# Key copies by GpSimd, sums of weight quarters kept in DRAM, and four more products in plain float32, in a decoder-layer kernel

## The chip, the cores and the metric

The kernel runs on one core of one Trainium2 chip. The metric is device time in microseconds (us) of one launch; lower is better. The result must agree with a float32 reference.

## The reference, cut to what matters

One layer over 2048 tokens of width 1024, all in float32. `IN_COLS` is 3072, `HEAD_DIM` 64, `D_FF` 4096.

```python
def hybrid_mixer(h, w_in, conv_w, g_attn_out, g_conv_out, w_out):
    proj = h @ w_in
    q, k, v, bg, cg, xc = jnp.split(proj, 6, axis=-1)          # 8 heads of 64
    for window, dilation in ((128, 1), (512, 4), (2048, 16)):
        o, lse = dilated_window_attention(q, k, v, window, dilation)
        outs.append(o); lses.append(lse)
    mix_w = jax.nn.softmax(jnp.stack(lses, axis=0), axis=0)
    attn = jnp.einsum('pbsh,pbshe->bshe', mix_w, jnp.stack(outs, axis=0))
    conv = short_gated_conv(bg, cg, xc, conv_w)
    return jnp.concatenate([rms_norm(attn), rms_norm(conv)], -1) @ w_out
# x += hybrid_mixer(rms_norm(x)); x += memory_cross_attention(rms_norm(x), mem)
# x += squared_relu(rms_norm(x) @ w_up) @ w_down; final rms_norm
```

Every query attends, in each of the three patterns, to a band of keys in its own block and in the block before. The three outputs are mixed by a softmax over the logarithms of their denominators.

## The kernel before, in words

**Products of matrices.** The large products are cut into *groups*, one for a weight block of 1024x1024 and one half of the tokens (1024). A group does 7 products of quarters instead of 8 (a Strassen-Winograd scheme): some of its operands are sums or differences of quarters. Each product is 4 *steps*, one for each tile of 128 rows, so a group has 28 steps. The order of the products in a group is 1, 2, 6, 7, 4, 5, 3. Group names: -2 to 3 are the input projection (`vg`, `ux`, `qk` for the first token half, then the same three for the second), 6 and 7 are `w` (the output projection), 8 and 9 are `s`, 10 and 11 are `o`, 12 and above are the MLP. Groups of one weight block for the two token halves (-2 and 1, -1 and 2, 0 and 3, 6 and 7, 10 and 11) have the same left operand; 8 and 9 have the same right operand, which is computed.

**Split and plain steps.** In a split step each operand is cut into a high part (by ScalarE: `w_hi` L206, `o_hi` L271) and the remainder (by VectorE: `w_lo` L213, `o_lo` L282), and TensorE does 12 matmuls of 128x512 in a fast float32 form (L385; L380 where two tiles of 256 are done). A product in the table `WHOLE` does 4 matmuls in plain float32 instead (L401, or L397) and needs no cut; the profile records each of these as two rows. Before the change `WHOLE` holds products 1 and 2 of group -2.

**Sums of quarters.** `w_sum` (L215 to L226) and `o_sum` (L228 to L244) form them on VectorE, in each group anew, each over 128x1024, into the loaded page or into a small buffer. `w_load` (L166 to L180) loads the four quarters of a group's weights, a page each of [128, 4, 512] (1 MB), from a ring of 20 pages.

**Order.** The tables `WSUM` and `OSUM` and the lists `plan` and `post` say before or after which step each such job is written; each engine then runs what was written for it in that order. `later(d, job)` writes a job d *ticks* on; there is a tick after each step and, in attention, after each unit. All transfers are issued by SyncE (SP), in the order in which they were written.

**Attention** (from L744) runs between groups 3 and 6: 4 pairs of heads, for each pair the patterns 2, 1, 0 and for each pattern 16 units, so 48 units a pair. A unit makes scores (matmuls L790 and L791, which read query pages and key pages), masks (VectorE L802), exponentials (ScalarE L813), transposes (L830) and outputs (L847). `qk` writes the loads of the next pair: `load_q` L703, `load_k` L726 to L731, `load_v` L736. A key page holds the same 64 rows twice, in partitions 0 to 63 and 64 to 127, since the high and low parts of the queries stand in the two halves. `load_k` fetches them twice from DRAM (L729 and L731, 512 KB each); only for pair 0 the second half is a VectorE copy (`dup_k` L734). `order_q` (L709) copies queries into the order of another pattern, on GpSimd (POOL, L717), ScalarE or VectorE.

**Combination.** After a pair, `combine` mixes its three outputs while the next pair runs: weights are computed (L893 to L902), stored to DRAM (`btd`, L905), loaded back broadcast over partitions for each quarter `tb` of the tokens (L927, L928), and GpSimd does five products and sums of 128x512 for each quarter (L917); the result is stored by `dma` L422. The delays are those of `combine`, L933 to L945.

Of the kernel before, what the change touches and what calls it, by code (L numbers as in the profile page):

```python
# [50 lines left out]
def _body(tc, a, out):  # L51
# [108 lines left out]
    WHOLE = {(-2, 1), (-2, 2)}  # L160
# [21 lines left out]
    def w_src(g, p, m):  # L182
        if p in (6, 3):
            return S2_[m // 2][:, m % 2]
        return WQ[g, *{1: (0, 0), 2: (0, 1), 7: (0, 0), 4: (1, 1), 5: (1, 0)}[p]][:, m]
# [41 lines left out]

    def o_sum(g, i, m):  # L228
# [15 lines left out]
        dve.tensor_tensor(to, x, y, op)  # L244

    def o_src2(g, p, m):
        if KEEP[g] and p in (7, 4, 5):
# [4 lines left out]

    def o_hi(o, m):
# [772 lines left out]
    for j in range(16):  # L1026
# [440 lines left out]
```

## Time and profile before

| | before |
|---|---|
| median of 3 runs | 2682.17 us (2678.83 to 2685.64) |
| profiled execution | 2685.0 us, its span 2682.8 us |
| TensorE busy | 2614.5 us, 97% |
| VectorE busy | 2259.4 us, 84% |
| ScalarE busy | 1458.1 us, 54% |
| GpSimd busy | 116.6 us, 4% |

A share of 97% says that TensorE has work nearly always; it is an average over stages. Where it falls in one stage, the timeline of TensorE (PE) shows the gap and, in brackets behind a row, how long the engine was idle and which instruction ended the wait. PEclk is the clock that TensorE was granted, as a share of full speed. DMA share is the mean busy share of the 16 DMA engines. A step's time is the distance between the starts of its first matmul and the next step's.

### The profile page before, as it was taken

To read this page: it belongs to the slowest core of one execution; us is meant where nothing else is said; L and a number is where in the kernel's file an instruction comes from. 1 tells how busy PE (TensorE), PEld (TensorE's weight loads), DVE (VectorE), ACT (ScalarE), POOL (GpSimd) and SP (SyncE) were. 2 spreads that over 40 slices of the span, in tenths; PEclk is the share of its full clock that TensorE was granted. 3 is DMA by queue.
4 is the path that set the end of the run, shared out by engine and by line. 5 is a ranking of instruction groups with operands and counts; after the bars stand their busy time and mean duration, and the time that the engine had idled before them with its cause. 6 is when DMAs were issued, how large, how long until landed. Compare 5 with 4: busy or idle time off the path is not lost.

```text
span 2682.8 us, 35255 instructions
## 1 busy us (share of the span) xinstructions
PE 2614.5 (97%) x13350; PEld 2171.2 (81%) x13350; DVE 2259.4 (84%) x3469; ACT 1458.1 (54%) x2466; POOL 116.6 (4%) x133
## 2 busy tenths in 40 slices
PE   8999999989889999999999999999999999999998
PEld 6888888878778677888888888888887888888886
DVE  6989889768676699998999887879789987978788
ACT  5545555358666344677545546364554636355563
POOL 0000000001344200000000000000000000000000
PEclk9999999999989999999999999999999999999999
DMA  4736443895787944355563211111121511111111
GB/s 162 232 104 210 153 166 134 269 262 119 178 186 220 306 166 158 110 188 189 205 218 110 95 63 63 63 63 63 48 94 48 188 63 64 63 33 55 56 47 63
DMA packets 196680, 353.91 MB, mean 132 GB/s; under 512 B 21024, under 2 KB 76704, under 8 KB 186912
## 3 DMA queue, kind: packets, MB, share of 16 engines
q1 hardware_dynamic: 195968, 351.15, 41.6%
q8 instruction: 105, 1.72, 0.3%
q14 instruction: 63, 0.52, 0.1%
q10 hardware_dynamic: 544, 0.52, 0.1%
HBM read 264.53 MB, written 87.10 MB: 131 GB/s over the span
## 4 chain that ended last, share of the span: by engine, by line
PE 63%; DVE 22%; DMA 9%; issue 3%; ACT 2%; SPq 1%; POOL 1%; DVEq 0%; ACTq 0%; POOLq 0%
PE ps L385 54%; DVE pg L282 4%; DVE w L213 4%; DMA w<-btd 2%; DMA pg<-qkd 2%; PE ps L847 2%; PE ps L380 1%; DVE s L39 1%; PE ps L790 1%; PE ps L830 1%; DVE pg L1089 1%; PE ps L791 1%; DVE pg L244 1%; PE ps L112 1%; DVE pg L219 1%
## 5 line engine op out<-in xcount | busy, mean ns | idle before, releaser
L385 PE MATMUL ps<-pg,w 128*128 128x512 f32 x9036 | 2080.8, 391 | 20.7 <-DVE pg L282 16.2
L385 PEld LDWEIGHTS ps<-pg,w 128*128 128x128 f32 x9036 | 1692.2, 188 | 380.0 <-DVE pg L282 25.0
L206 ACT ACTIVATE w<-pg 128x1024 fp32r<-128x1024 f32 x276 | 290.9, 1054 | 271.4 <-PE ps L385 235.9
L282 DVE TENSOR_TENSOR pg<-pg 128x1024 fp32r<-128x1024 f32 x308 | 375.2, 1220 | 3.6 <-ACT pg L271 3.2
L213 DVE TENSOR_TENSOR w<-pg,w 128x1024 fp32r<-128x1024 f32 x276 | 336.5, 1219 | 47.6 <-ACT w L206 47.3
L271 ACT ACTIVATE pg<-pg 128x1024 fp32r<-128x1024 f32 x308 | 314.1, 1046 | 37.4 <-DVE pg L500 13.3
L813 ACT ACTIVATE s<-s,stat 128x256 f32<-128x256 f32 (+1 forms) x384 | 172.6, 451 | 75.5 <-DVE stat L802 75.0
L1212 DVE TENSOR_TENSOR pg<-ps,pg 128x512 f32<-128x512 f32 x223 | 151.8, 684 | 49.0 <-PE ps L385 49.0
L206 ACT ACTIVATE w<-s 128x1024 fp32r<-128x1024 f32 x112 | 117.9, 1053 | 134.4 <-PE ps L385 78.3
L412 ACT ACTIVATE s<-pg 128x1024 f32<-128x1024 f32 x79 | 83.3, 1056 | 186.1 <-DVE pg L1089 111.4
L802 DVE CUSTOM_DVE_ANT_0 s<-ps,w 128x256 f32<-128x256 f32 (+1 forms) x344 | 108.9, 370 | 47.9 <-PE ps L791 42.6
L213 DVE TENSOR_TENSOR w<-s,w 128x1024 fp32r<-128x1024 f32 x112 | 136.1, 1215 | 2.4 <-ACT w L206 2.4
L244 DVE TENSOR_TENSOR pg<-pg 128x1024 f32<-128x1024 f32 x112 | 136.3, 1217 | 1.0
L1183 DVE TENSOR_TENSOR pg<-ps,pg 128x512 f32<-128x512 f32 x96 | 65.9, 687 | 77.6 <-PE ps L385 77.6
L790 PE MATMUL ps<-pg 128*128 128x256 f32 x384 | 108.3, 313 | 10.8 <-DMA pg<-qkd 8.9
L791 PE MATMUL ps<-pg 128*128 128x256 f32 x384 | 98.4, 287 | 12.1 <-DMA pg<-qkd 8.4
L1184 ACT ACTIVATE pg<-pg 128x512 f32<-128x512 f32 x96 | 60.6, 631 | 80.9 <-DVE pg L1183 80.8
L1178 ACT ACTIVATE pg<-ps 128x512 f32<-128x512 f32 x96 | 56.7, 596 | 86.1 <-PE ps L385 85.5
L282 DVE TENSOR_TENSOR pg<-s,pg 128x1024 fp32r<-128x1024 f32 x78 | 94.5, 1219 | 9.7 <-ACT pg L271 9.6
L833 DVE COPY s<-ps 128x256 f32<-128x256 f32 (+1 forms) x192 | 100.9, 566 | 1.3 <-PE ps L830 0.7
L271 ACT ACTIVATE pg<-s 128x1024 fp32r<-128x1024 f32 x78 | 82.0, 1052 | 33.2 <-DVE s L244 33.2
L790 PEld LDWEIGHTS ps<-pg 128*128 128x128 f32 x384 | 73.7, 192 | 27.2 <-issue 15.1
(158 smaller groups left out, 2422.8 us busy)
## 6 DMA issues: line engine op xcount, KB each, us to landing
pg<-w_up SPq DMA_DIRECT2D x32, 1024.0 KB
pg<-w_down SPq DMA_DIRECT2D x32, 1024.0 KB
pg<-qkd SPq DMA_DIRECT2D x44, 512.0 KB
pg<-w_in SPq DMA_DIRECT2D x21, 1024.0 KB
pg<-xT SPq DMA_DIRECT2D x19, 1024.0 KB
qkd<-pg SPq DMA_DIRECT2D x64, 256.0 KB
pg<-x2d SPq DMA_DIRECT2D x16, 1024.0 KB
vd<-pg SPq DMA_DIRECT2D x96, 128.0 KB
```

The costliest lines, as they stand in the source:

```text
L206: act.activation(hi, src, AF.Copy)
L213: dve.tensor_tensor(lo, src, f(hi), OP.subtract)
L244: dve.tensor_tensor(to, x, y, op)
L271: act.activation(hi, src, AF.Copy)
L282: dve.tensor_tensor(lo, src, f(hi), OP.subtract)
L385: pe.matmul(ps, wt[l][:, m % 2, k * 128:k * 128 + 128], o[x][:, k, cols], start=k == 0 and j == 0 and p in (1, 2, 5), stop=k == 3 and j == ...
L790: pe.matmul(Sh, qv, kv[0], start=True, stop=False)
L791: pe.matmul(Sh, qv, kv[1], start=False, stop=True)
L802: dve.tensor_tensor_reduce(smv, sv, mv, -0.125, 3e38, OP.add, OP.min, mt[:, c1:c1 + 1])
L813: act.activation(pout, pin, AF.Exp, bias=mt[:, c1:c1 + 1], scale=-1.0, accum_out=zt[:, c1:c1 + 1])
L833: dve.tensor_copy(t_.rearrange("p i h q -> p (i h q)")[:, :w], pt[:, :w])
L1212: dve.tensor_tensor(y, ps, y, OP.add)
```

## The change

Four things are changed.

1. **Sums kept in DRAM.** For the groups in `LSUM` (keys: the second token half; values: the first) and `RSUM` (group 9 from 8), the first group stores the four sums of quarters (`smd`, 1 MB for each) as it forms them, and the second group loads seven pages, one for each product (`s_load`, `t_load`), instead of four, and forms no sums of that operand. 24 MB are stored and 24 sum pages loaded more; 18 more pages in all, as 6 quarters are no longer needed. 48 VectorE sums (40 in `w_sum`, 8 in `o_sum`) are gone.
2. **Plain float32.** `WHOLE` takes in (0, 2), (6, 2), (6, 4) and (19, 4): 16 steps. Their cuts, 4 on VectorE and 4 on ScalarE for each product, are gone.
3. **Keys.** For pairs 1 to 3 a key page is loaded once, into partitions 0 to 63, and GpSimd copies it into the other half in four pieces of 64x512, written 6 ticks after the load. The four key loads are written at (pattern 1, units 5, 12, 15) and (pattern 0, unit 1) instead of (1, 10), (1, 13), (0, 1), (0, 4); the queries at (2, 12) instead of (1, 2); the values of the next pair's first pattern at (0, 6) instead of (1, 2).
4. **Combination.** Its delays are shorter: weights at 7, 8, 9 instead of 8, 10, 12, store at 10 instead of 14, loads of quarter `tb` at 11 + 5 tb instead of 15 + 5 tb, the products 3 ticks behind their loads instead of 2, the stores 11 + tb instead of 8.

Line numbers behind the change: L385 is L416, L401 is L433, L206 is L205, L213 is L212, L271 is L298, L282 is L309, L244 is L264, L219 is L218, L717 is L750, L917 is L954, L927 is L964, L729 is L762, L738 is L773, L422 is L455; the copy of keys is L769.

```diff
+    LSUM, RSUM = {1: -2, 2: -1, 3: 0, 7: 6, 11: 10}, {9: 8}
+    smd = {g: {p: dp.tile([128, 4, 512], F32, name=f"smd{g + 2}_{p}") for p in ((4, 5, 6, 7) if g == 8 else (3, 5, 6, 7))} for g in (-2, -1, 0, 6, 8, 10)}
...
-    WHOLE = {(-2, 1), (-2, 2)}
+    WHOLE = {(-2, 1), (-2, 2), (0, 2), (6, 2), (6, 4), (19, 4)}
...
     def w_src2(g, p, m):
+        if g in LSUM and p in (6, 7, 5, 3):
+            return WQ[g, p][:, m:m + 2]
...
+        if g in LSUM.values():
+            if i in (2, 4):
+                later(1, dma, smd[g][6 if i == 2 else 3][:, 2 * m:2 * m + 2], S2_[m])
+            elif m == 1:
+                later(1, dma, smd[g][7 if i == 3 else 5], WQ[g, 0, 0] if i == 3 else WQ[g, 1, 0])
+
+    def s_load(g, p):
+        if p in (1, 2, 4):
+            w_load(g, *{1: (0, 0), 2: (0, 1), 4: (1, 1)}[p])
+        else:
+            WQ[g, p] = page([128, 4, 512])
+            sp.dma_start(WQ[g, p], smd[LSUM[g]][p])
...
+            if g + 1 in LSUM:
+                for i, p in enumerate(order):
+                    after(28 * g + 18 + 4 * i, s_load, g + 1, p)
+            else:
+                for d, q in ((13, (0, 0)), (19, (1, 1)), (21, (1, 0)), (22, (0, 1))):
+                    after(28 * g + d, w_load, g + 1, *q)
...
         sp.dma_start(f(t_[0:64]), src)
-        if pr:
-            sp.dma_start(f(t_[64:128]), src)
-
-    def dup_k(h, i):
-        dve.tensor_copy(K[0, h, i][64:128], f(K[0, h, i][0:64]))
+
+    def dup_k(pr, h, i, eng=pool):
+
+        t_ = K[pr, h, i]
+        for b in range(1 if eng is dve else 4):
+            cs = slice(0, T) if eng is dve else slice(b * 512, b * 512 + 512)
+            eng.tensor_copy(t_[64:128, cs], f(t_[0:64, cs]))
...
-        kj = {(1, 10): 0, (1, 13): 1, (0, 1): 2, (0, 4): 3}.get((pat, b))
+        kj = {(1, 5): 0, (1, 12): 1, (1, 15): 2, (0, 1): 3}.get((pat, b))
         if kj is not None and pr < 3:
             load_k(pr + 1, kj // 2, kj % 2)
+            later(6, dup_k, pr + 1, kj // 2, kj % 2)
...
-            later((4, 5, 5)[i] if last else 8 + 2 * i, comb_w, pr, i, eng)
-        later(6 if last else 14, comb_bt, pr)
+            later((4, 5, 5)[i] if last else 7 + i, comb_w, pr, i, eng)
+        later(6 if last else 10, comb_bt, pr)
...
-                later(15 + 5 * tb, comb_ldb, pr, tb, pool, 2, 8)
+                later(11 + 5 * tb, comb_ldb, pr, tb, pool, 3, 11 + tb)
```

On GpSimd, while pair 1 runs and the keys of pair 2 come, the last two quarters of the combination of pair 0 (`w_...` are the broadcast weights) stand before the change ahead of the reordering of queries for pair 2:

```order
L917 TENSOR_TENSOR pg<-pg,w_5879 128x512 x2
L917 TENSOR_TENSOR pg<-pg 128x512
L917 TENSOR_TENSOR pg<-pg,w_5880 128x512
L917 TENSOR_TENSOR pg<-pg 128x512
L917 TENSOR_TENSOR pg<-pg,w_5979 128x512 x2
L917 TENSOR_TENSOR pg<-pg 128x512
L917 TENSOR_TENSOR pg<-pg,w_5980 128x512
L917 TENSOR_TENSOR pg<-pg 128x512
L717 CAST pg<-pg 128x4x4x32 x6
```

Behind it the same place reads, from the copies of the first key page on:

```order
L769 CAST pg<-pg 64x512 x4
L954 TENSOR_TENSOR pg<-pg,w_5783 128x512 x2
L954 TENSOR_TENSOR pg<-pg 128x512
L954 TENSOR_TENSOR pg<-pg,w_5784 128x512
L954 TENSOR_TENSOR pg<-pg 128x512
L954 TENSOR_TENSOR pg<-pg,w_5887 128x512 x2
L954 TENSOR_TENSOR pg<-pg 128x512
L954 TENSOR_TENSOR pg<-pg,w_5888 128x512
L954 TENSOR_TENSOR pg<-pg 128x512
L769 CAST pg<-pg 64x512 x12
L750 CAST pg<-pg 128x4x4x32 x6
```

The copies of the other three key pages stand behind the last products and ahead of the queries' reordering.

On SP, in the same pair, the key loads stand before between the loads of the third and fourth quarter of the combination and behind a store of its result (L422):

```order
L729 DMA pg<-qkd 64x2048
L731 DMA pg<-qkd 64x2048
L422 DMA atd<-pg 128x512
L927 DMA w_5979<-btd 64x2x512
L928 DMA w_5980<-btd 64x512
L927 DMA w_5979<-btd 64x2x512
L928 DMA w_5980<-btd 64x512
L729 DMA pg<-qkd 64x2048
L731 DMA pg<-qkd 64x2048
L422 DMA atd<-pg 128x512
L729 DMA pg<-qkd 64x2048
L731 DMA pg<-qkd 64x2048
```

Behind the change:

```order
L455 DMA atd<-pg 128x512
L964 DMA w_5887<-btd 64x2x512
L965 DMA w_5888<-btd 64x512
L964 DMA w_5887<-btd 64x2x512
L965 DMA w_5888<-btd 64x512
L762 DMA pg<-qkd 64x2048
L455 DMA atd<-pg 128x512
L762 DMA pg<-qkd 64x2048 x2
L455 DMA atd<-pg 128x512
L773 DMA pg<-vd 128x16x128
```

The last two key loads stand behind the store of the second quarter's result, where before one pair of them stood behind that of the third.

On VectorE, early in group 1 (`vg` of the second token half), the first sums of quarters (L219, L222) stand before among the cuts:

```order
L605 TENSOR_TENSOR pg<-ps,pg 128x512
L213 TENSOR_TENSOR w_2013<-pg,w_2012 128x2x4x128
L219 TENSOR_TENSOR pg<-pg 128x1024
L495 SCALAR_TENSOR_TENSOR pg<-pg,g_mix,s_1769 128x512 x2
L605 TENSOR_TENSOR pg<-ps,pg 128x512
L222 TENSOR_TENSOR s_2061<-pg 128x1024
L495 SCALAR_TENSOR_TENSOR pg<-pg,g_mix,s_1769 128x512 x2
```

Behind the change:

```order
L638 TENSOR_TENSOR pg<-ps,pg 128x512
L212 TENSOR_TENSOR w_2005<-pg,w_2004 128x2x4x128
L528 SCALAR_TENSOR_TENSOR pg<-pg,g_mix,s_1761 128x512 x2
L638 TENSOR_TENSOR pg<-ps,pg 128x512
L528 SCALAR_TENSOR_TENSOR pg<-pg,g_mix,s_1761 128x512 x2
```

The two sums are gone from between the cuts, and nothing stands in their place.

## Rows read from the trace of the kernel before

**Rows 1.** The page, busy time of each engine: us (share of the span) and instructions.

```profile
PE 2614.5 (97%) x13350; PEld 2171.2 (81%) x13350; DVE 2259.4 (84%) x3469; ACT 1458.1 (54%) x2466; POOL 116.6 (4%) x133
```

**Rows 2.** Busy time of each engine in the stretches of head pairs 1, 2 and 3: start and end, length, then us and count for each engine, granted clock, DMA share, GB/s.

```profile
634.70:699.70 65.00, 64.73 (x647) 56.18 (x645) 56.57 (x250) 53.29 (x210) 22.96 (x27) 1.00 0.77 169
699.70:775.60 75.90, 67.92 (x646) 58.48 (x644) 55.78 (x250) 53.04 (x210) 31.77 (x37) 0.93 0.79 181
775.60:851.80 76.20, 66.65 (x633) 57.86 (x632) 55.05 (x247) 52.41 (x206) 36.10 (x41) 0.91 0.72 181
```

**Rows 3.** Timeline of PE at the beginnings of pairs 1, 2 and 3: start, duration, line, count; in brackets the idle time before and what ended it. The rows of each pair are the first matmul of its first unit, the waits, and the first matmul of its third unit.

```profile
634.68 0.39 PE L790 MATMUL ps<-pg 128*128 128x256 f32 x1
...
637.73 0.38 PE L790 MATMUL ps<-pg 128*128 128x256 f32 x1
...
699.67 0.39 PE L790 MATMUL ps<-pg 128*128 128x256 f32 x1
...
703.52 0.58 PE L790 MATMUL ps<-pg 128*128 128x256 f32 x1 [3.35 <-DMA pg<-qkd]
708.56 0.55 PE L791 MATMUL ps<-pg 128*128 128x256 f32 x1 [4.46 <-DMA pg<-qkd]
...
713.50 0.39 PE L790 MATMUL ps<-pg 128*128 128x256 f32 x1
...
775.64 0.39 PE L790 MATMUL ps<-pg 128*128 128x256 f32 x1
...
791.23 0.58 PE L790 MATMUL ps<-pg 128*128 128x256 f32 x1
```

**Rows 4.** The chain of waits that ends in the first unit of pair 2: start, duration, what (SPq is SP's issue of a DMA).

```profile
696.41 0.32 SPq L422
...
697.35 11.08 DMA pg<-qkd
```

**Rows 5.** Timeline of POOL in pair 1, where the combination of pair 0 is computed, columns as in rows 3.

```profile
663.37 2.70 POOL L917 TENSOR_TENSOR pg<-pg,w 128x512 f32<-128x512 f32 x2 [10.37 <-DMA w<-btd]
...
704.41 1.26 POOL L917 TENSOR_TENSOR pg<-pg 128x512 f32<-128x512 f32 x1
705.74 3.40 POOL L717 CAST pg<-pg 128x512 fp32r<-128x512 f32 x6
```

**Rows 6.** Busy time by stretch, columns as in rows 2: 500 to 520 us, with transfers over all 128 partitions, and 540 to 553 us, with loads of keys and queries into 64 partitions.

```profile
500.00:520.00 20.00, 20.00 (x93) 17.36 (x92) 11.51 (x21) 6.27 (x9) 0.00 (x0) 1.00 1.02 337
540.00:553.00 13.00, 13.00 (x62) 11.44 (x61) 4.29 (x9) 3.13 (x7) 2.67 (x4) 1.00 1.03 215
```

**Rows 7.** Busy time by stretch, columns as in rows 2: a stretch of the MLP with split steps only.

```profile
1510.30:1967.30 457.00, 457.00 (x2018) 378.41 (x2017) 373.10 (x379) 244.95 (x300) 0.00 (x0) 1.00 0.17 58
```

**Rows 8.** Timeline of PE in group -2, columns as in rows 3: two plain float32 steps of 8 recorded rows each, and what follows.

```profile
21.79 7.03 PE L401 MATMUL ps<-pg 128*128 128x512 f32 x16
28.66 7.07 PE L397 MATMUL ps<-pg 128*128 128x256 f32 x32
```

**Rows 9.** The page, costliest groups of instructions, one of sums of quarters: line, engine, tiles and shapes, count, busy us, mean ns of one, idle time before and what ended most of it.

```profile
L244 DVE TENSOR_TENSOR pg<-pg 128x1024 f32<-128x1024 f32 x112 | 136.3, 1217 | 1.0
```

**Rows 10.** Timeline of PE in group 1, columns as in rows 3: the starts of two times two steps, and the waits in them.

```profile
271.14 0.39 PE L385 MATMUL ps<-pg,w 128*128 128x512 f32 x1
273.85 5.95 PE L385 MATMUL ps<-pg,w 128*128 128x512 f32 x23 [2.32 <-DVE pg L282]
279.63 5.99 PE L380 MATMUL ps<-w,pg 128*128 128x256 f32 x48
285.46 0.39 PE L385 MATMUL ps<-pg,w 128*128 128x512 f32 x1
...
293.22 5.92 PE L380 MATMUL ps<-w,pg 128*128 128x256 f32 x48
```

**Rows 11.** Busy time by stretch, columns as in rows 2: the part of group 1 that holds rows 10; single long steps of groups 6 and 7 and the stretch around them; two long steps of groups 19 and 20.

```profile
259.90:290.50 30.60, 26.42 (x158) 22.68 (x158) 30.50 (x33) 14.55 (x18) 0.00 (x0) 1.00 0.36 121
...
915.70:1101.20 185.50, 174.90 (x791) 143.48 (x790) 178.01 (x225) 74.92 (x81) 10.45 (x8) 0.95 0.58 193
...
945.25:954.75 9.50, 5.08 (x13) 3.25 (x12) 9.46 (x11) 3.06 (x3) 0.00 (x0) 0.70 0.00 0
1014.30:1018.30 4.00, 2.99 (x13) 2.16 (x13) 3.83 (x10) 2.01 (x2) 0.00 (x0) 1.00 0.00 0
1027.20:1034.80 7.60, 4.62 (x12) 3.45 (x13) 7.57 (x9) 3.82 (x6) 0.00 (x0) 0.78 1.01 322
2046.20:2050.70 4.50, 3.33 (x14) 2.13 (x13) 4.50 (x6) 2.01 (x2) 0.00 (x0) 1.00 0.00 0
2058.90:2064.70 5.80, 4.95 (x29) 3.79 (x28) 5.76 (x7) 3.56 (x6) 0.00 (x0) 1.00 0.00 0
```

**Rows 12.** Timeline of DVE and PE, columns as in rows 3: a VectorE wait in group 0 and PE's 16 short matmuls of a normalization in group 20.

```profile
192.96 0.69 DVE L605 TENSOR_TENSOR pg<-ps,pg 128x512 f32<-128x512 f32 x1 [2.96 <-PE ps L385]
...
2063.00 1.84 PE L112 MATMUL ps<-ones,s 128*128 128x1 f32 x16
```

**Rows 13.** Timeline of SP and ACT in group 2, columns as in rows 3: two loads of 1 MB (`ud`) and the instruction that waits for them.

```profile
352.20 1.28 SPq L613 DMA_DIRECT2D pg<-ud  x2
...
363.37 0.72 ACT L634 ACTIVATE pg<-pg,conv_w 128x512 f32<-128x512 f32 x1 [3.85 <-DMA pg<-ud]
```

**Rows 14.** Instructions of one line, VectorE's reordering of queries: duration in ns (least, median, most).

```profile
L724 DVE CAST pg<-pg x16: 415/418/1411, 589.5 to 821.1; 128x512 fp32r<-128x512 f32 x16
```

More of the change, by code (lines that the diff above doesn't have):

```diff
@@ L180, in w_load @@
             sp.dma_start(t_, a[src][r + 4 * i:r + 4 * i + 4, :, j * 512:j * 512 + 512].rearrange("m p c -> p m c"))
[L182 to L185, printed above, removed]
     def w_src2(g, p, m):
+        if g in LSUM and p in (6, 7, 5, 3):
+            return WQ[g, p][:, m:m + 2]
         if p in (6, 3):
@@ L226, in w_sum, with t_load @@
             dve.tensor_tensor(S2_[m], a12, S2_[m], OP.subtract)
+        if g in LSUM.values():
[9 more added lines that the diff above has]
+            sp.dma_start(WQ[g, p], smd[LSUM[g]][p])
+    def t_load(g, p):
+        if p in (1, 2, 3):
+            b_load(g, *{1: (0, 0), 2: (1, 0), 3: (1, 1)}[p])
+        else:
+            BQ[g][p] = page([128, 4, 512])
+            sp.dma_start(BQ[g][p], smd[RSUM[g]][p])
     def o_sum(g, i, m):
@@ L244, in o_sum @@
         dve.tensor_tensor(to, x, y, op)
+        if g in RSUM.values() and m == 1:
+            later(1, dma, smd[g][{3: 7, 2: 6, 4: 4, 1: 5}[i]], BQ[g][{3: (0, 1), 4: (1, 0)}.get(i, (0, 0))])
     def o_src2(g, p, m):
+        if g in RSUM and p in (6, 7, 4, 5):
+            return BQ[g][p][:, 2 * m:2 * m + 2]
         if KEEP[g] and p in (7, 4, 5):
@@ L257, in o_hi @@
         if (g, p) in WHOLE:
+            if g > -2:
+                OP_[o] = [o_src2(g, p, m_)[:, j] for m_ in range(2) for j in range(2)]
+                return
             if m == 0:
@@ L327, in _body @@
         if KIND[g]:
-            for fn, tab in ((w_sum, WSUM[KEEP[g]]), (o_sum, OSUM[KEEP[g]])):
+            for fn, tab in ((w_sum, WSUM[KEEP[g]] if g not in LSUM else {}), (o_sum, OSUM[KEEP[g]] if g not in RSUM else {})):
                 for i, ds in tab.items():
@@ L340, in _body @@
         if KIND[g] and g + 1 < NS_ and KIND[g + 1]:
-            for d, q in ((13, (0, 0)), (19, (1, 1)), (21, (1, 0)), (22, (0, 1))):
-                after(28 * g + d, w_load, g + 1, *q)
+            if g + 1 in LSUM:
+                for i, p in enumerate(order):
+                    after(28 * g + 18 + 4 * i, s_load, g + 1, p)
+            else:
+                for d, q in ((13, (0, 0)), (19, (1, 1)), (21, (1, 0)), (22, (0, 1))):
+                    after(28 * g + d, w_load, g + 1, *q)
     def ahead(n):
@@ L392, in whole_mm @@
         g, x = n // 28, OP_[n // 4]
-        for t in range(2 if m > 1 else 1):
+        first = p in (1, 2, 5)
+        for t in range(2 if g == -2 and m > 1 else 1):
             for k in range(4):
-                if m > 1:
+                if g == -2 and m > 1:
                     b = 2 * m - 4 + t
@@ L400, in whole_mm @@
                 else:
-                    pe.matmul(ps, w_src(g, p, m)[:, k * 128:k * 128 + 128], x[:, k], start=k == 0, stop=k == 3)
+                    pe.matmul(ps, w_src2(g, p, m // 2 * 2)[:, m % 2, k * 128:k * 128 + 128], x[:, k] if g == -2 else x[k],
+                              start=first and k == 0, stop=k == 3, skip_group_check=True)
         return ps
@@ L762, in qk @@
             load_v(pr, 0)
-        if pat == 1 and b == 2 and pr < 3:
+        if (pat, b) == (2, 12) and pr < 3:
             load_q(pr + 1)
+        if (pat, b) == (0, 6) and pr < 3:
             load_v(pr + 1, 2)
@@ L1042, in _body @@
         if j in (10, 11, 12, 13):
-            dup_k((j - 10) // 2, (j - 10) % 2)
+            dup_k(0, (j - 10) // 2, (j - 10) % 2, dve)
         tick()
@@ L1249, in _body @@
     for g in range(8, 12):
-        for d, q in ((19, (0, 0)), (20, (1, 0)), (22, (1, 1)), (23, (0, 1))):
-            after(28 * (g - 1) + d, b_load, g, *q)
+        if g in RSUM:
+            for i, p in enumerate(order):
+                after(28 * g - 10 + 4 * i, t_load, g, p)
+        else:
+            for d, q in ((19, (0, 0)), (20, (1, 0)), (22, (1, 1)), (23, (0, 1))):
+                after(28 * (g - 1) + d, b_load, g, *q)
     XLD = {(0, 0): 4, (1, 0): 6, (1, 1): 12, (0, 1): 13}
```

## The prediction, as it was written before the result

> **What bounds the kernel now.** I read the page first, then the stretches, then the timelines. The page shows TensorE busy for 97% of the span [rows 1]: 2682.8 - 2614.5 = 68.3 us are all that waits can give back, unless matmuls themselves become fewer or faster. So I look for where these 68 us lie. In the MLP they are nowhere: 457 us of split steps without a gap, 2018 matmuls in them, so 457 / (2018 / 12) = 2.72 us a step [rows 7]; VectorE has 84 us to spare there. Two places show gaps that the change touches.
>
> The first is the change from one head pair to the next. Pairs 1, 2 and 3 do the same 48 units in 65.0, 75.9 and 76.2 us [rows 2]. The first two units take 637.73 - 634.68 = 3.05 us in pair 1, 713.50 - 699.67 = 13.83 in pair 2 and 791.23 - 775.64 = 15.59 in pair 3 [rows 3]: all of the difference is here, 10.8 + 12.5 = 23.3 us. In brackets stand two waits for a DMA of keys; what remains beside them is matmuls at half clock (the mean granted clock of these pairs is 0.93 and 0.91 against 1.00). The chain says why the keys are late: GpSimd's products release the store of a quarter (L422), which SP issues at 696.41; the last key load stands behind it and lands 11.08 us after 697.35 [rows 4]. The pair had ended at 699.67.
>
> The second is a few stretches of matrix products where VectorE is never idle: in group 1 it is busy 30.50 of 30.60 us, in groups 6 and 7 178.0 of 185.5, and the long steps have it at 9.46 of 9.50, 7.57 of 7.60, 4.50 of 4.50 [rows 11]. There PE waits for the cut L282 [rows 10].
>
> **The change, part by part.** The sum is made against the profiled execution, 2685.0 us, which is 2.8 above the median of the runs.
>
> *Keys and combination.* Each pair's keys lose four loads of 512 KB, 2 MB. While loads run in 64 partitions all DMA engines are occupied (1.03) for 215 GB/s, against 337 GB/s at 1.02 over 128 [rows 6]; 2 MB at 215 GB/s is 9.8 us of all engines, in pairs that use them at 0.77 and 0.79 [rows 2]. A tick is 65.0 / 48 = 1.354 us. The combination starts four ticks earlier, 5.4 us, though its first loads now stand behind those of the queries; I put GpSimd's first products at about 664, as before (663.37), and its four quarters without the gaps that it now has: one quarter is five instructions of about 1.3 us [rows 5], 6.5 us. Four quarters are 26 us. The copies are new: 16 a pair of 64x512. No row shows one. The nearest is the reordering of queries, 3.40 / 6 = 0.57 us for 128x512 [rows 5]; a copy of half the partitions may cost anything from half of that, 0.28 us, to a product's 1.3 us. I take 0.57, since each partition has as many elements: 16 x 0.57 = 9.1 us. Then the last copy ends at 664 + 26 + 9.1 = 699.1, against the pair's end at 699.67: just in time. At 1.3 us each it would be 711, at 0.28 694.6. Of the 23.3 us I leave 1 us for each of the two changes of pair, 2 us, and 1 us because VectorE's copies of queries sometimes meet GpSimd (418 ns as a rule, 1411 once [rows 14]). Attention: -23.3 + 2 + 1 = -20.3 us. The bounds: -23.3, and, if GpSimd keeps today's pace, its last product ends at 704.41 + 1.26 = 705.67 [rows 5], 12 copies of 0.57 behind it make 712.5, which is 4.1 us later than today's 697.35 + 11.08 = 708.43, so +8.2 us for two changes. The change into pair 1 waits for nothing now (3.05 us) and has the same slack.
>
> The Trainium skill, "SBUF — State Buffer", section "Door 1: The DMA port swizzle (why `[64,N]` ≈ `[32,N]`)", says that a transfer into 64 partitions reaches only half of the 16 ports, and gives about 196 against 328 GB/s for 1 MiB. The trace agrees in kind (215 against 337). By that rule the change keeps the slow half-width form for every key load and halves only their number, so the landing of a single load is no quicker; alone it would leave the last keys late, which is the first rival below.
>
> *Plain float32.* Two plain steps take 28.66 - 21.79 = 6.87 us [rows 8], 3.43 a step, against 2.72 [rows 7]: +0.71 for each of 16 steps, +11.4 us of TensorE, 2.84 for each product. On VectorE each product frees four cuts of 1.22 us [rows 9], 4.9 us. In group 0 that frees nothing: VectorE waits there for PE (2.96 us at 192.96 [rows 12]); +2.8, between 0 and +2.8. The others stand with the sums.
>
> *Sums.* 48 sums of 1.217 us [rows 9] are 58.4 us less of VectorE. What that is worth is the PE gap where they lay. Group 1: two pairs of steps take 279.63 - 271.14 = 8.49 and 293.22 - 285.46 = 7.76 [rows 10] instead of 5.44; gaps of 3.05 and 2.32, together 5.4. VectorE has four sums before the second, 4 x 1.22 = 4.9: -4.9, between -5.4 and 0. Groups 6 and 7: three steps take 9.5, 4.0 and 7.6 us [rows 11], so gaps of 6.8, 1.3 and 4.9, together 12.9 us. There VectorE loses 8 cuts and 8 sums, 19.5 us, and the gaps go: -12.9 + 5.7 for (6, 2) and (6, 4) = -7.2 us, between -7.2 and +5.7. The lower clock in two of these steps (0.70, 0.78) came with the waits and goes with them. Group 19: steps of 4.5 and 5.8 us [rows 11], the second with 1.8 us of short matmuls [rows 12]; gaps of 1.8 and 1.3, against +2.8 for (19, 4): -0.3, between -0.3 and +2.8. In groups 3, 9 and 11 PE has no gap of this kind, so their sums give nothing.
>
> *More transfers.* 24 MB stored and 18 MB loaded more are 42 MB; at 337 GB/s that is 125 us of all DMA engines, spread over stretches at a share of 0.2 to 0.6 (0.36 in group 1, 0.58 in groups 6 and 7 [rows 11]). Hidden, where a load is in time. Each sum page is issued five steps, 13.6 us, before its first use. In group 2 the `ud` loads now have a sum page of 1 MB ahead of them on SP, 3.1 us at that rate, and ScalarE already waits for them (3.85 us [rows 13]): +1, between 0 and +4.
>
> The sum: -20.3 + 2.8 - 4.9 - 7.2 - 0.3 + 1 = -28.9, so 2685.0 - 28.9 = 2656.1, and less 2.8 for the median: **2653**.
>
> **Rivals.**
>
> *A: the copies come as late as the loads do now.* GpSimd is behind the broadcast loads, which still fill the DMA engines, and its chain ends where it does now. For it: gaps of some 10 us before each quarter (10.37 [rows 5]). Against: these loads have 2 MB less beside them and start four ticks earlier. Attention then gives 0 and the rest -8.6: 2685.0 - 8.6 - 2.8 = 2673.6. Chance 0.15.
>
> *B: slower, by the way over DRAM.* A sum page is loaded after both halves were stored, in the same SP queue, behind everything that waits there. The point is a landing of 13.6 us after issue; the nearest row, two loads of 1 MB, took 363.37 - 352.20 = 11.2 us [rows 13], and a key load 11.08. At 16.6 us each of 24 pages makes its product wait 3 us: +72, 2653 + 72 = 2725. Against: they are fewer than the DMA engines can carry in most groups. Chance 0.05.
>
> *C: VectorE's gaps stay.* The steps wait for an order, not for VectorE's total: then only the +11.4 us are paid, with -20.3 and +1: 2685.0 - 7.9 - 2.8 = 2674.3. Against: VectorE is full in all of these stretches. Chance 0.08.
>
> *D: everything goes.* Attention -23.3, and the removed work also closes the small gaps around these steps, some 10 us: 2685.0 - 42 - 2.8 = 2640. Chance 0.1.
>
> **How the numbers follow.** My forecast has 0.62, with a range of its own of 2645 to 2665. Less than 0.3% (8 us, what a measurement of this kernel can hardly tell from none) ends at 2674. Rivals A and C lie on that edge: half of each counts as no change. Faster 0.62 + 0.1 + 0.115 = 0.835, of which I give 0.005 away to mishaps: 0.83; no change 0.115; slower 0.055, rival B and what I have not thought of. The range reaches from D's end to A's: 2641 to 2674.
>
> **What would show it.** Right: the first two units of pairs 2 and 3 take 3 to 5 us, the pairs 65 to 67; PE has no wait for a copy of keys; the long steps of groups 1, 6 and 7 take 2.7 us, or 3.4 where plain; split steps at 2.72 elsewhere. Wrong: waits of PE for the copies (L769), or of the cuts for pages of `smd`; plain steps longer than 3.43; gaps in groups 6 and 7 with VectorE idle beside them.

## The result, and the profile after

The changed kernel takes 2668.71 us (median of 6, 2665.86 to 2672.99) against 2683.9 for the kernel before beside it: ratio 0.9942, 95% interval 0.9928 to 0.9956, so 15.2 us faster. The forecast, 2653, had the sign and twice the size. The profiled execution takes 2672.2 us, its span is 2670.4, 12.4 less than before.

The page after, busy time by engine, answers to [rows 1]: VectorE has 71 us less to do, GpSimd 27 more, and TensorE 8 us more, where the plain steps alone were to add 11.4.

```profile
PE 2622.3 (98%) x13286; PEld 2158.6 (81%) x13286; DVE 2188.5 (82%) x3405; ACT 1443.3 (54%) x2450; POOL 144.1 (5%) x181
```

The starts of each group's first matmul, in both timelines of PE, cut the span into stages (us):

| stage | before | after | change | forecast |
|---|---|---|---|---|
| group -1 | 76.8 | 84.0 | **+7.2** | 0 |
| group 0 | 80.8 | 83.7 | +2.9 | +2.8 |
| group 1 | 86.0 | 81.0 | -5.0 | -4.9 |
| group 2 | 80.2 | 81.1 | +0.9 | +1 |
| group 3 to the start of pair 0 | 133.6 | 135.8 | +2.2 | 0 |
| pair 0 | 75.0 | 73.3 | -1.7 | 0 |
| pairs 1 to 3 | 217.1 | 208.9 | **-8.2** | -20.3 |
| from there to group 6 | 63.9 | 62.2 | -1.7 | 0 |
| groups 6 and 7 | 185.5 | 178.5 | -7.0 | -7.2 |
| groups 8 to 18 | 866.1 | 864.7 | -1.4 | 0 |
| groups 19 and 20 | 163.1 | 163.7 | +0.6 | -0.3 |
| all else | 654.8 | 653.5 | -1.3 | 0 |

Not every row can be read to a microsecond. The kernels of combination_only and moves_only (below) run the instructions of the kernel before up to pair 0, and group 2 takes 82.0 and 80.5 us in them, group 3 to the start of pair 0 142.1 and 140.4. So the changes of group 2, of group 3 and of pair 0 are within what single executions differ by, and that group 2 meets its forecast is luck. The first three steps of group 6 differ in the same way (12.3 to 16.4 us in executions of the same steps; 15.5 before, 16.2 after); without them groups 6 and 7 change by -7.8. The rows of groups 0, 1, 8 to 18, 19 and 20 repeat within 0.5 us from run to run, where the kernels do not differ in them.

The matrix products came out term by term. Two rows are far off, group -1 and the pairs. Busy time by stretch for pairs 1 to 3 after (columns as in [rows 2]) shows pair 3 at its 64 us, but pair 1 now 8 us longer than it was and pair 2 only 4 us shorter:

```profile
640.20:713.40 73.20, 68.36 (x647) 58.38 (x645) 55.51 (x250) 53.29 (x210) 40.44 (x53) 0.95 0.72 163
713.40:784.90 71.50, 67.83 (x647) 58.42 (x645) 55.32 (x250) 53.24 (x210) 41.06 (x54) 0.95 0.73 166
784.90:849.10 64.20, 64.06 (x632) 55.55 (x632) 54.34 (x247) 52.42 (x206) 29.34 (x32) 1.00 0.75 217
```

The waits for keys at the beginnings of pairs [rows 3] are gone: the first two units of pairs 2 and 3 take 3.05 us each time. The time is lost inside the pair. The chain of waits after, from 699 us on (start, duration, what):

```profile
699.78 1.27 POOL pg L954
701.05 0.02 issue
701.07 0.60 ACT pg L896
701.67 0.50 ACT s L850 x2
702.16 0.04 issue
702.21 0.48 PE ps L867
```

and the same place in the timelines of ACT, PE and POOL (columns as in [rows 3]):

```profile
701.07 0.60 ACT L896 ACTIVATE pg<-ps 128x512 f32<-128x512 f32 x1 [6.80 <-POOL pg L954]
...
702.21 2.38 PE L867 MATMUL ps<-ident,s 128*128 128x128 f32 x8 [3.99 <-ACT s L850]
...
675.38 2.54 POOL L954 TENSOR_TENSOR pg<-pg,w 128x512 f32<-128x512 f32 x2 [16.17 <-DMA w<-btd]
...
703.67 6.77 POOL L769 CAST pg<-pg 64x512 fp32r<-64x512 f32 x12
```

ScalarE's L896 copies an output of pattern 0 out of PSUM into a page. It waits 6.80 us for a GpSimd product of the combination (L954) that has nothing to do with that output. ScalarE's exponentials (L850) stand behind it, and TensorE waits for these. GpSimd itself is late: its first product starts at 675.38, which is 35.2 us after the pair's start at 640.2; before, it was 663.37 - 634.70 = 28.7 [rows 2, 5].

In group -1 two steps take 5.8 and 6.2 us in place of 2.7. The timelines of PE, ACT and SP there:

```profile
115.28 0.80 PE L416 MATMUL ps<-pg,w 128*128 128x512 f32 x1 [2.92 <-ACT pg L298]
...
113.22 1.06 ACT L205 ACTIVATE w<-pg 128x1024 fp32r<-128x1024 f32 x1 [11.51 <-DMA pg<-w_in]
...
104.65 0.53 SPq L182 DMA_DIRECT2D pg<-w_in  x1
```

The last quarter of the group's weights is issued at 104.65. In the kernel before SP issued it at 97.16 (timeline of SP):

```profile
97.16 0.72 SPq L180 DMA_DIRECT2D pg<-w_in  x1
```

That stretch, by busy time (columns as in [rows 2]), had the DMA engines at 0.88 before the change already, and the 10 us ahead of it at 0.94:

```profile
80.00:90.00 10.00, 10.00 (x64) 9.04 (x64) 9.36 (x13) 5.86 (x9) 0.00 (x0) 1.00 0.94 297
90.00:100.00 10.00, 10.00 (x64) 9.04 (x64) 9.97 (x13) 5.62 (x8) 0.00 (x0) 1.00 0.88 291
```

After, the 10 us from 90 on (DMA share 0.97, 341 GB/s) have the stores of group -2's sums in them, as have the 20 us ahead:

```profile
90.00:100.00 10.00, 10.00 (x64) 9.04 (x64) 9.97 (x12) 5.58 (x8) 0.00 (x0) 1.00 0.97 341
```

### The profile page after: what moved, and what is told of

It reads as the page before. It is cut to its first block, busy times and chain, and to the rows that moved or that the text cites. A ratio compares the mean times of both kernels' runs of the same rounds, so it can differ in the third digit from the quotient of the medians.

```text
span 2670.4 us, 35198 instructions
## 1 busy us (share of the span) xinstructions
PE 2622.3 (98%) x13286; PEld 2158.6 (81%) x13286; DVE 2188.5 (82%) x3405; ACT 1443.3 (54%) x2450; POOL 144.1 (5%) x181
## 4 chain that ended last, share of the span: by engine, by line
PE 81%; DVE 9%; DMA 6%; ACT 2%; issue 1%; POOL 1%; SPq 1%; DVEq 0%; POOLq 0%; ACTq 0%
PE ps L416 65%; PE ps L884 3%; PE ps L867 2%; PE ps L433 2%; PE ps L827 2%; PE ps L411 1%; DMA pg<-qkd 1%; PE ps L828 1%; DVE pg L309 1%; DVE w L212 1%; PE ps L114 1%; DMA bgd<-pg 1%; PE ps L1060 1%; PE ps L1331 1%; POOL pg L954 1%
## 5 line engine op out<-in xcount | busy, mean ns | idle before, releaser
L416 PE MATMUL ps<-pg,w 128*128 128x512 f32 x8844 | 2033.3, 391 | 10.7 <-DVE pg L309 4.9
L416 PEld LDWEIGHTS ps<-pg,w 128*128 128x128 f32 x8844 | 1655.1, 188 | 359.8 <-DVE pg L309 10.5
L205 ACT ACTIVATE w<-pg 128x1024 fp32r<-128x1024 f32 x288 | 303.4, 1053 | 283.1 <-PE ps L416 237.6
L212 DVE TENSOR_TENSOR w<-pg,w 128x1024 fp32r<-128x1024 f32 x288 | 351.8, 1222 | 57.0 <-ACT w L205 56.4
L309 DVE TENSOR_TENSOR pg<-pg 128x1024 fp32r<-128x1024 f32 x300 | 365.0, 1217 | 5.0 <-ACT pg L298 4.6
L298 ACT ACTIVATE pg<-pg 128x1024 fp32r<-128x1024 f32 x300 | 305.8, 1046 | 29.2 <-DVE pg L264 11.3
L850 ACT ACTIVATE s<-s,stat 128x256 f32<-128x256 f32 (+1 forms) x384 | 172.6, 451 | 48.8 <-DVE stat L839 47.3
L205 ACT ACTIVATE w<-s 128x1024 fp32r<-128x1024 f32 x92 | 96.9, 1053 | 123.4 <-PE ps L416 74.7
L264 DVE TENSOR_TENSOR pg<-pg 128x1024 f32<-128x1024 f32 x104 | 126.7, 1218 | 1.5 <-DMA pg<-ptd 0.6
L212 DVE TENSOR_TENSOR w<-s,w 128x1024 fp32r<-128x1024 f32 x92 | 111.9, 1217 | 2.5 <-ACT w L205 2.4
L1221 ACT ACTIVATE pg<-pg 128x512 f32<-128x512 f32 x96 | 60.6, 631 | 80.9 <-DVE pg L1220 80.8
L309 DVE TENSOR_TENSOR pg<-s,pg 128x1024 fp32r<-128x1024 f32 x78 | 94.5, 1220 | 9.7 <-ACT pg L298 9.6
L39 DVE TENSOR_TENSOR s<-s,s 128x1024 f32<-128x1024 f32 x56 | 69.2, 1236 | 31.5 <-ACT s L445 31.5
L867 PE MATMUL ps<-ident,s 128*128 128x128 f32 x600 | 86.4, 279 | 8.8 <-ACT s L850 8.3
```

The lines of the kernel that those rows point to most:

```text
L205: act.activation(hi, src, AF.Copy)
L212: dve.tensor_tensor(lo, src, f(hi), OP.subtract)
L298: act.activation(hi, src, AF.Copy)
L309: dve.tensor_tensor(lo, src, f(hi), OP.subtract)
L416: pe.matmul(ps, wt[l][:, m % 2, k * 128:k * 128 + 128], o[x][:, k, cols], start=k == 0 and j == 0 and p in (1, 2, 5), stop=k == 3 and j == ...
L850: act.activation(pout, pin, AF.Exp, bias=mt[:, c1:c1 + 1], scale=-1.0, accum_out=zt[:, c1:c1 + 1])
```

## The experiments

The first four runs stand on the changed kernel (2668.7) and test what ate the gain. Theory: a page that is reused too soon, queries ahead of the broadcasts, and stores ahead of a weight load. Each has its rival in its expectation.

**pages_free.** The last quarter's products are written 4 ticks later, so that the allocation of the new output's page finds another one.

```diff
-                later(11 + 5 * tb, comb_ldb, pr, tb, pool, 3, 11 + tb)
+                later(11 + 5 * tb, comb_ldb, pr, tb, pool, 7 if tb == 3 else 3, 11 + tb + (4 if tb == 3 else 0))
```

> The changed kernel, with the last quarter's products of the combination written 4 ticks later, so that the page of the new output (pattern 0) is no longer one that these products release; two of the four key copies stay behind them. Page theory (ScalarE's wait of 6.8 us for GpSimd in units 10 and 11 of pattern 0 is a page that was reused): this wait is gone in pairs 1 and 2, those two units take about 6.1 us in place of 9.4 + 3.9; but the last copies still end some 70 us after the pair's start, so PE now waits 4 to 6 us for them at the start of pairs 2 and 3; pairs 1 and 2 take 69 to 72 us with what follows, and the whole is 2 to 6 us faster than the changed kernel (2668.7). Rival (ScalarE is slowed by GpSimd as such): the wait stays, no change.

Measured: 2669.01 us (ratio to before 0.9945, 0.9927 to 0.9962). ScalarE's wait is gone, and units 10 to 13 of pattern 0 take 6.1 us, in place of 9.4 + 3.9 (the "two units" of the expectation are two pairs of them). Pairs 1 to 3 take 65.6, 66.5 and 66.9 us, 9.9 less in all than in the changed kernel. PE's waits by releaser (us in total, times, longest) name the copies now, which end behind the pair:

```profile
PE ps L828 <- POOL pg L769: 3.5, 2, 1.8
```

That settles the page: GpSimd does the same work, and ScalarE no longer waits. But the whole is no faster, against what I expected. In its profile, 7.8 us were lost ahead of pair 0, most of them between group 3 and pair 0, where no instruction differs. That stretch is looked at below (best_a, best_b). Why the median of four runs shows nothing of the 9.9 us stays open.

**copies_first.** As before, 8 ticks: all copies of keys stand ahead of the last quarter's products.

```diff
+                later(11 + 5 * tb, comb_ldb, pr, tb, pool, 11 if tb == 3 else 3, 11 + tb + (8 if tb == 3 else 0))
```

> The changed kernel, with the last quarter's products 8 ticks later, so behind all copies of keys. Page theory: neither the page nor the copies are late; the copies end some 64 us after the pair's start; pairs 1 and 2 take 65 to 67 us in place of 73.2 and 71.5, the first units of pairs 2 and 3 no wait; some 12 to 14 us faster than the changed kernel, so 2655. Rival (GpSimd disturbs ScalarE): no change.

Measured: 2654.27 us (0.989, 0.9875 to 0.9905), 14.4 less than the changed kernel. Busy time of pairs 1 to 3 by stretch, and then POOL's timeline in pair 1:

```profile
639.90:705.60 65.70, 65.19 (x647) 56.33 (x645) 55.27 (x250) 53.27 (x210) 33.39 (x44) 1.00 0.72 162
705.60:770.20 64.60, 64.54 (x647) 56.16 (x645) 55.12 (x250) 53.22 (x210) 41.09 (x54) 1.00 0.78 184
770.20:834.10 63.90, 63.82 (x632) 55.50 (x632) 54.36 (x247) 52.41 (x206) 36.42 (x41) 1.00 0.78 243
```

```profile
696.68 6.75 POOL L769 CAST pg<-pg 64x512 fp32r<-64x512 f32 x12
703.50 2.52 POOL L954 TENSOR_TENSOR pg<-pg,w 128x512 f32<-128x512 f32 x2
```

The copies end at 703.4, before the pair does at 705.6, and PE is busy throughout, with the full clock. So GpSimd as such does not hold up the pair: it is busy for 41 of 64.6 us in pair 2. Single VectorE instructions do get longer: of the 16 that reorder queries in this run (duration in ns, least, median, most), three take 685 to 889 ns in place of some 418, each beside GpSimd instructions. The pairs do not show it:

```profile
L757 DVE CAST pg<-pg x16: 415/418/889, 594.5 to 803.3; 128x512 fp32r<-128x512 f32 x16
```

**queries_early.**

```diff
-        if (pat, b) == (2, 12) and pr < 3:
+        if (pat, b) == (2, 0) and pr < 3:
             load_q(pr + 1)
```

> The changed kernel, with the queries of the next pair loaded at the pair's start (pattern 2, unit 0) in place of unit 12. Theory that the queries' 2 MB ahead of the first broadcast loads make GpSimd's products late (they start 35.2 us after the pair's start, 28.7 before the change): they start at 28 to 30, the page is released 6 us earlier, ScalarE's wait shrinks from 6.8 to under 1 us, and the copies end before the pair does: 12 to 14 us faster, 2655. Rival (products late because of the store and load of the weights before them): products still start at 34 to 36, no change.

Measured: 2658.63 us (0.9902, 0.9882 to 0.9922); pairs 65.9, 64.6 and 64.1. Pair 1 starts at 640.5, and POOL's first product comes 27 us later, with half the wait for its broadcasts:

```profile
667.45 2.52 POOL L954 TENSOR_TENSOR pg<-pg,w 128x512 f32<-128x512 f32 x2 [8.45 <-DMA w<-btd]
```

So the queries, 2 MB ahead of the first broadcasts, made GpSimd some 8 us late. With it in time, the page is free when ScalarE wants it.

**stores_late.** Two of group -2's four sums are stored behind the last weight load of group -1.

```diff
-                later(1, dma, smd[g][6 if i == 2 else 3][:, 2 * m:2 * m + 2], S2_[m])
+                later(9 - 2 * m if g == -2 and i == 4 else 1, dma, smd[g][6 if i == 2 else 3][:, 2 * m:2 * m + 2], S2_[m])
             elif m == 1:
-                later(1, dma, smd[g][7 if i == 3 else 5], WQ[g, 0, 0] if i == 3 else WQ[g, 1, 0])
+                later(11 if g == -2 and i == 1 else 1, dma, smd[g][7 if i == 3 else 5], WQ[g, 0, 0] if i == 3 else WQ[g, 1, 0])
```

> The changed kernel, with the stores of two of the four sums of group -2 (2 MB, those for products 5 and 3) written behind the last weight load for group -1. Theory that these stores hold up that load in a stretch where the DMA engines are full (0.97): the load is issued 6 us earlier, the two steps of 5.8 and 6.2 us in group -1 take 2.7, group -1 77 us in place of 84; 7 us faster than the changed kernel, 2662. Rival (the DMA engines are full anyway, it comes from the sums of group -1 or the copies of v): half or none of it.

Measured: 2663.76 us (0.9924, 0.9909 to 0.9938), 5 us less than the changed kernel. The two intervals overlap, so the profile has to decide. SP, ACT and PE at the place:

```profile
97.13 0.74 SPq L182 DMA_DIRECT2D pg<-w_in  x1
...
106.60 1.06 ACT L205 ACTIVATE w<-pg 128x1024 fp32r<-128x1024 f32 x1 [4.20 <-DMA pg<-w_in]
...
101.97 26.42 PE L416 MATMUL ps<-pg,w 128*128 128x512 f32 x113
```

The load is back at 97.13 and PE runs through. Group -1 takes 76.8 us again, and 78.4 and 78.6 in best_a and best_b, which have these late stores too; in the other seven profiles of the changed kernel and its variants it takes 82.8 to 85.1.

**plain_undone.** `WHOLE` is `{(-2, 1), (-2, 2)}` again.

> The changed kernel with the 16 new plain float32 steps as split steps again. Theory that plain steps pay only where VectorE has no time left: groups 0 and 19 gain the 2.8 us each that they paid; in groups 6 and 7 VectorE gets 9.7 us of cuts back and gaps of 4 to 8 us return, so that these two come out level or up to 2 us slower or faster; group 20's first step is 4.5 us again. Together 2 to 6 us faster than the changed kernel (2663 to 2667). Rival (the sums in DRAM alone were enough): no gap returns, 11 us faster, 2657. Rival (the plain steps were what removed the gaps): 3 us slower or more.

Measured: 2668.09 us (0.9941, 0.9926 to 0.9956): no difference from the changed kernel that these runs could tell. By stages: group 0 takes 80.8 us (-2.9), group 19 78.9 (-2.9), group 20 84.2 (+2.3). Groups 6 and 7 by stretch, first as changed, then with the plain steps undone:

```profile
911.30:1008.70 97.40, 95.07 (x392) 69.11 (x390) 85.73 (x118) 29.89 (x34) 8.15 (x5) 0.96 0.65 225
1008.70:1089.80 81.10, 80.43 (x370) 66.45 (x369) 71.78 (x92) 37.58 (x40) 0.00 (x0) 1.00 0.74 246
```

```profile
907.70:1002.30 94.60, 88.74 (x424) 73.08 (x422) 92.32 (x119) 37.06 (x41) 6.08 (x5) 0.98 0.66 229
1002.30:1085.60 83.30, 80.75 (x370) 66.42 (x369) 73.80 (x99) 37.91 (x40) 0.00 (x0) 1.00 0.71 240
```

Undone, PE has 5.9 and 2.6 us of gaps there; with the plain steps 2.3 and 0.7, and more to compute. By these sums the two plain products of group 6 cost what they save: 178.5 against 177.9 us. Without the first three steps of group 6, which differ between executions, it is 162.2 to 162.3 us in all nine profiles with these two products and the sums of group 7, and 163.3 undone: there they gain 1.1 us. In group 0 the plain product only costs, and that of group 19 costs 0.6 us more than it saves in group 20.

**sums_of_two_groups.** `LSUM` is `{1: -2, 7: 6}` and `RSUM` is empty.

> The changed kernel with sums kept in DRAM only for groups 1 and 7 (from -2 and 6), where VectorE had no idle time; groups 2, 3, 9 and 11 form them again. Theory: those four gave nothing (no gap of PE before), so their steps stay at 2.72 us, and the transfers that go (16 MB stored, 12 MB loaded) give back part of what group -1 and group 2 lost: 0 to 5 us faster than the changed kernel. Rival (they gave something that the gaps did not show): slower by 2 us or more.

Measured: 2669.69 us (0.9949, 0.9934 to 0.9964), the same within the intervals. What the sums of the other four groups give and what their transfers cost can't be told from the medians. The profiles show a little: groups 8 to 18 take 864.6 to 864.7 us in all eight kernels that have these sums and 866.1 to 866.2 in all six that do not, 0.4 us of it in group 9 and 1.1 in group 12.

**keys_twice.** On copies_first: keys by DMA again, without copies.

```diff
         sp.dma_start(f(t_[0:64]), src)
+        if pr:
+            sp.dma_start(f(t_[64:128]), src)
...
-            later(6, dup_k, pr + 1, kj // 2, kj % 2)
```

> The kernel of copies_first (2654.3), with every key page loaded twice from DRAM as before the change and no copies by GpSimd. Theory that the DMA engines, full from the 20th to the 60th us of a pair, are what the copies relieve: 2 MB more a pair push the last keys to 5 to 12 us behind the pair's end; pairs 2 and 3 begin with waits for a DMA of 4 to 10 us each, 10 to 20 us slower, 2664 to 2674. Rival (the earlier place of the loads alone does it): no wait, 2654.

Measured: 2659.63 us (0.9905, 0.9889 to 0.9922). My theory fell: no pair begins with a wait for keys, though the DMA engines work more (0.94 against 0.78 in pair 2):

```profile
642.20:708.20 66.00, 65.22 (x649) 56.31 (x645) 55.27 (x250) 53.29 (x210) 31.95 (x37) 1.00 0.79 182
708.20:773.40 65.20, 65.03 (x647) 56.36 (x645) 55.20 (x250) 53.34 (x210) 32.11 (x37) 1.00 0.94 214
773.40:837.90 64.50, 64.27 (x634) 55.61 (x634) 55.33 (x249) 52.45 (x207) 28.87 (x31) 1.00 0.86 260
```

The three pairs take 195.7 us, against 194.2 with copies. The other 4 us of the two medians, whose intervals overlap, do not come from the pairs. So what relieved the keys? Three runs on the kernel before take the parts singly.

**combination_only, moves_only, moves_and_combination.** The kernel before with the new delays of `combine` (part 4); with the new places of the loads (part 3 without the copies); with both.

> The kernel before with the combination's new delays alone (part 4). Theory that the key loads were late because SP held them behind the stores of the combination's result: those stores are now written later, so the key loads no longer stand behind the third; but the queries' loads still come between the first and the second quarter's broadcasts. The first two units of pairs 2 and 3 fall from 13.8 and 15.6 us to 3 to 8 us; 10 to 22 us faster than before, 2661 to 2673. Rival (the keys' own late place decides): no change.

> The kernel before with the new places of the loads alone (queries, keys, values; every key page still loaded twice, no copies, old delays of the combination). Same theory: the last keys are written 3 units earlier and stand ahead of the third store; first two units of pairs 2 and 3 3 to 5 us; 18 to 23 us faster than before, 2660 to 2666. Rival: the queries' loads ahead of the first broadcasts make GpSimd and its stores later, the keys behind them too: 10 us or less.

> The kernel before with the new places of the loads and the new delays of the combination, but no copies by GpSimd, no sums in DRAM, no new plain steps. By keys_twice no copy is needed and no page of the combination's is waited for: pairs 1, 2 and 3 take 65 to 66 us each, 22 us faster than before, 2661 to 2663. Rival (the copies are needed): pairs 2 and 3 begin with waits of 4 us or more, 2666 or more.

Measured: 2683.12 us (0.9989, 0.9976 to 1.0003); 2676.22 (0.9969, 0.9958 to 0.998); 2661.43 (0.9914, 0.9897 to 0.9932). The first is no change that can be told, the second 8 us or so, both together 23. My expectations for the single parts were too high. In the profiles the first two units of pairs 2 and 3 take 11.9 and 13.5 us with the combination alone, 10.9 and 12.0 with the moves alone (13.8 and 15.6 before), and 3.05 with both. The last keys for pair 2 show why. Counted from the start of pair 1, SP issues the last of their loads after 62.7 us before the change (697.35 [rows 4] - 634.70 [rows 2]), 57.5 with the combination alone (702.68 - 645.14), 57.1 with the moves alone (697.27 - 640.13) and 49.6 with both (688.00 - 638.41). Each part alone gains some 5 us, and the load still lands 7.1 and 5.8 us behind the end of its pair (8.8 before). With the combination alone the chain into pair 2 goes back to the landing of a broadcast load of the last quarter; the second chain is that with the moves alone:

```profile
693.35 9.31 DMA w<-btd
702.66 0.02 issue
702.68 14.74 DMA pg<-qkd
```

```profile
697.27 12.93 DMA pg<-qkd
710.20 0.14 issue
710.33 0.55 PE ps L792
```

With both (SP's timeline, then busy time by stretch), the last keys are issued at 688.00 in a pair that ends at 703.0, and the pairs take their 65 us, without any copy:

```profile
688.00 0.44 SPq L731 DMA_DIRECT2D pg<-qkd  x1
```

```profile
638.40:703.00 64.60, 64.55 (x646) 56.21 (x644) 55.21 (x250) 53.24 (x210) 32.03 (x37) 1.00 0.81 185
703.00:767.80 64.80, 64.68 (x646) 56.16 (x644) 55.99 (x250) 53.24 (x210) 32.18 (x37) 1.00 0.94 218
767.80:833.00 65.20, 64.81 (x634) 55.61 (x632) 54.94 (x247) 52.53 (x206) 28.92 (x31) 1.00 0.83 249
```

By the medians these two parts alone are 7 us faster than the whole change.

**best_a, best_b.** best_a is copies_first with stores_late and without the plain steps of groups 0 and 19. best_b also leaves out the copies and the sums in DRAM of groups 2, 3, 9 and 11.

> The kernel of copies_first with the late stores of group -2 and without the plain steps of groups 0 and 19. If the parts add up: 2654.3 - 5 to 7 - 4 to 6 = 2642 to 2646. If they take one from the other: 2648 or more.

> The kernel of best_a (2649.6) without what the runs showed to give nothing: no copies of keys by GpSimd (every key page loaded twice), and sums kept in DRAM only for groups 1 and 7. If the copies and the other four groups' sums are worth nothing: 2646 to 2652, the same. If they carry something that the single runs did not show: 2655 or more.

Measured: 2649.55 us (0.9873, 0.9858 to 0.9888) and 2649.77 (0.9873, 0.9857 to 0.989). Both are 34 us faster than before and 19 faster than the changed kernel, and they are equal: copies of keys and the sums of four groups carry nothing that the medians show. The parts did not add up to the 2642 to 2646 of the expectation. One reason is in plain_undone: giving up the plain steps of groups 0 and 19 is worth 2.9 + 0.6 = 3.5 us, not 4 to 6. Another may lie in a stretch that no run shortens, between group 3 and pair 0, by busy time of 490 to 520 us before, after and in best_b:

```profile
490.00:520.00 30.00, 30.00 (x137) 25.62 (x137) 21.47 (x35) 9.96 (x13) 0.00 (x0) 1.00 1.01 327
```

```profile
490.00:520.00 30.00, 30.00 (x136) 25.39 (x135) 23.73 (x37) 11.12 (x15) 0.00 (x0) 1.00 0.98 307
```

```profile
490.00:520.00 30.00, 30.00 (x140) 25.92 (x139) 15.95 (x27) 7.72 (x11) 0.00 (x0) 1.00 1.02 339
```

The DMA engines are full there in all of them. Group 3's start to the third unit of pair 0 took 147.8 us before, 148.4 after, 148.8 in copies_first, 150.5 in best_a, 153.0 in stores_late and 157.5 in pages_free. But it took 156.8 in combination_only, whose instructions up to there are those of the kernel before. So it differs by 9 us between executions without any change, and one profile of each kernel can't show whether what is won ahead of that stretch is lost in it. That a transfer limits it is likely from the shares; it was not tried, and what else the parts take from one another stays open.

## Why the prediction was right, and where it was not

*Plain float32 and sums: right, term by term.* Group 0 paid 2.9 us (2.8 forecast); one row shows its four plain steps at 13.89 / 4 = 3.47 us each:

```profile
196.22 13.89 PE L433 MATMUL ps<-pg 128*128 128x512 f32 x32
```

Group 1 gained 5.0 (4.9), groups 6 and 7 7.0 (7.2; 7.8 without the first three steps of group 6), groups 19 and 20 lost 0.6 (0.3 gained by the forecast). Reading a gap of PE beside a VectorE without idle time, and crediting the removed work only up to that gap, gave good sums. Rival C (the gaps stay) is refuted by these rows. What I had not asked is whether both means were needed in groups 6 and 7: plain_undone shows that the plain products gain only 1.1 us there. And "their sums give nothing", of groups 3, 9 and 11, is 1.4 us short: groups 8 to 18 gained that.

*Keys and combination: right about the wait that would go, wrong in two steps behind it.* The step that failed first is "I put GpSimd's first products at about 664, as before (663.37)". That is 29.3 us after the pair's start; they came at 35.2. With the queries out of the way (queries_early) they come at 26.9. So the four ticks gave 28.7 - 26.9 = 1.8 us and not 5.4, and the queries' four loads, which I named as standing ahead, took 35.2 - 26.9 = 8.3, where the forecast leaves them 6.0 (28.7 - 5.4 + 6.0 = 29.3). Four quarters without gaps (26 us forecast, 703.61 - 675.38 = 28.2 with the first copies among them) and 0.57 us a copy (6.77 / 12 = 0.564) were right. The copies therefore ended 70.2 us after the pair's start (703.67 + 6.77 - 640.2), between the 64.4 of the forecast (699.1 - 634.7) and the 77.8 of its bound for GpSimd at its old pace (712.5 - 634.7). The second is a wait that the prediction did not contain: a page which the moved products release later than a new output wants it. Not keys but ScalarE's copy of an output stopped the pair, 6.80 us. In pair 1 PE was idle for 4.8 us (73.20 - 68.36), and busy for 3.2 us longer than in copies_first (68.36 against 65.19), with a granted clock of 0.95 against 1.00. The time, 2668.7, lies nearer to rival A's 2673.6 than to the forecast, but not by A's mechanism, as no pair begins with a wait for keys. I followed the release of pages for the loads alone, and not for instructions of engines that write into a page.

*The reason for the gain was wrong.* I took the copies, 2 MB less in the DMA engines, to be what makes the keys come in time. keys_twice and moves_and_combination have no copies, all of the loads, and the same 65 us pairs. It is the place on SP: the last keys are issued 49.6 us after the pair's start in place of 62.7, once the loads and the combination are both moved. The Trainium skill, "SBUF — State Buffer", section "Door 1: The DMA port swizzle (why `[64,N]` ≈ `[32,N]`)", says that a transfer into 64 partitions reaches only half of the ports. I weighed that as a reason against the change, and no run contradicts it: the loads stay narrow, and with twice their number pair 2 of moves_and_combination has the DMA engines at 0.94 for 218 GB/s. But at their new place there is room for all of them. The 215 GB/s of [rows 6], from which I priced the saved loads, are no rate of narrow loads alone either: 419 - 82 = 337 of the 591 packets of that stretch hold 4 KB and belong to weight loads into all 128 partitions.

*More transfers: "Hidden, where a load is in time" failed in group -1.* The sum was made of shares of 0.36 and 0.58 in other groups. The stretch from 80 to 100 us had 0.88 to 0.94 already, and the row for it was not read. 2 MB of stores there took 7.5 us of the weights' lead (104.65 - 97.16). Rival B's mechanism, sum pages that come late, did not decide: of the 24 sum pages ScalarE waited for one, 3.5 us, and PE for none.

## What to carry to other kernels

When transfers are moved, follow not only the loads but every instruction that writes into a buffer of the same ring: a reuse that was free can become a wait on an engine that has nothing to do with either. Look at the order on the one queue that issues all transfers before counting bytes: here two moves together gave 23 us, each alone 0 to 8, and the saved 2 MB a pair nothing. Added stores need the DMA share of the very stretch in which they fall: here 2 MB of them, in a stretch at 0.88 to 0.94, made the load behind them 7.5 us later. And compare instructions of two runs by their distance from the start of the stage, not by the clock of the whole run: the stage itself has moved.

## What the runs showed of the hardware

GpSimd busy for 41 of 64.6 us did not lengthen the units beside it: pair 2 of copies_first takes 64.6 us, with PE busy for 64.54, and that of moves_and_combination, where GpSimd is busy for 32.2 us, 64.8 with 64.68. A GpSimd copy of 64x512 takes 0.56 us, as long as one of 128x512 (0.57 [rows 5]). That half the partitions save nothing is likely from this, but not shown: the longer one also changes the order of the elements.
